# A hybrid layer on one core: zeros and an earlier norm at the start, the delta rule's masks applied where products are read, side work ranked anew

## The chip, the cores and the metric

The kernel runs on one core of one Trainium2 chip. Time is in microseconds (us) of the device, for the whole program. PE multiplies matrices (PEld, its weight loads, is shown apart), DVE, ACT and POOL work on tiles in SBUF and PSUM, SP issues the weight DMAs. Each engine runs its own instructions in the order of the program and waits on semaphores for the others.

## The reference

Two blocks with fp32 data: x has 256 tokens of 1024 channels. The first block is the one that changes:

```python
def hybrid_layer(x, norm_mix_w, w_in, ...):
    h = rmsnorm(x, norm_mix_w)
    proj = jnp.einsum("bsd,de->bse", h, w_in)
    qkv, z, b_logit, a_logit, lru_x, lru_gate = jnp.split(proj, SPLIT_IDX, axis=-1)
    qkv = jax.nn.silu(causal_depthwise_conv(qkv, gdn_conv_w))
    q, k, v = jnp.split(qkv, 3, axis=-1)          # 4 heads of 128, q and k l2-normalised
    beta = jax.nn.sigmoid(b_logit)
    g = -jnp.exp(gdn_A_log) * jax.nn.softplus(a_logit + gdn_dt_bias)
    o = gated_delta_rule_chunked(q, k, v, g, beta)
    gdn_out = rmsnorm(o, gdn_norm_w) * jax.nn.silu(z)
    xr = causal_depthwise_conv(lru_x, lru_conv_w) + lru_conv_b
    lru_out = rg_lru(xr, ...) * jax.nn.gelu(lru_gate)   # two gates, then a scan over the tokens
    x = x + jnp.einsum("bse,ed->bsd", jnp.concatenate([gdn_out, lru_out], -1), w_out)
    ...                                            # MLP: w_ff1, relu squared, w_ff2
```

The delta rule solves a unit lower triangular system per chunk and head, then carries a state from chunk to chunk:

```python
    a_low = jnp.where(strict, jnp.einsum("bhnid,bhnjd->bhnij", k_beta, k) * decay, 0.0)
    sol = lax.linalg.triangular_solve(a_low + eye, rhs, left_side=True, lower=True)
    ...
        v_new = u_c - jnp.einsum("bhck,bhkv->bhcv", w_c, state)
        o_c = (jnp.einsum("bhck,bhkv->bhcv", q_c * jnp.exp(g_c)[..., None], state)
               + jnp.einsum("bhij,bhjv->bhiv", attn_c, v_new))
```

The second block has two layers of gated MLPs, attention and a convolution branch, and is the same before and after.

## The kernel before

Everything is held with channels on partitions and the 256 tokens along the row. A weight product is made of three fp32r matmuls per k-tile of 128 channels: rounded weights by rounded x (L552), rounded weights by x's rest (L553), the weights' rest by rounded x (L554), each 128x256. ACT makes the rounded weights (`wh`, from `raw`, which a DMA brings), DVE the rest (`wl` = raw - wh); a table, POOLED, gives the rests of some jobs to POOL. A job is one output tile of 128 channels; it has eight k-tiles, so 24 matmuls.

The first block has 24 jobs of w_in: ORDER1 takes four tiles each of k, q, x (the LRU's input), g (its output gate), v and z. That is matmuls 1 to 576 of the weight stream. w_out follows in two parts: o1a, the four k-tiles that the LRU's result feeds (eight jobs of 12 matmuls), and o1b, those that the delta rule feeds. Both add into the same banks of PSUM. Then come the MLP and block two.

All else runs beside the jobs as **flows**, Python generators that yield between pieces: conv and SiLU of each tile (`conv4`, `do_qkv`), `decays` (beta and decays from w_ba), `sums` and `factors` (norms of q and k), `chunk` (the inverse of the triangular matrix and the state, one flow for each of two chunks of 128 tokens), `sides` (scaled q, k, v for it), `lru` (gates, square root, scan). A planner keeps a clock for each engine (`clk`) and calls `tick` behind each k-tile of a job: a flow goes on when its event has come, in order of its rank, and one with a limit only while DVE's clock is less than the limit ahead of PE's (`ready`, L372). So the planner writes down one fixed order for each engine. `force` lets flows run on where a job needs something.

In `chunk` the inverse T is built by levels: in each a product M1 of the masked matrix and T, a product with T, an addition, a transposition and a copy; the last blocks are 32 and 64 wide. The masks are LM, the masked matrix NL is made by POOL at L1110 (512 columns, once in each of four levels and two chunks). `lru` turns each of four tiles into two gates by products with LG and five ACT instructions. At the end the squares of the outputs are summed (`sso`), and norm and z's gate follow.

At the start ACT rounds x, four of the squares of x are made by ACT and four by POOL, POOL adds the halves, PE sums the columns by products with `ones`, and `root_norm` gives `rc`. `wb` is w_ba rounded and its rest, for the 32 products that give beta and the decays' input.

Helpers record an operation under their own line: ACT at L295, DVE at L307 (two tensors), L312/L314 (a tensor and numbers), L318 (scalar, tensor, tensor), POOL at L330, PE at L338 (products) and L342 (transpositions).

## Time and profile before

| | |
|---|---|
| time, median of 3 runs | 1510.01 us (1508.57 to 1511.97) |
| the profiled execution's own time | 1510.12 us |
| its span, first to last instruction | 1508.4 us |
| mean granted clock of PE | 0.991 |
| PE busy | 1471.4 us (98%) |
| DVE busy | 1073.8 us (71%) |
| ACT busy | 800.6 us (53%) |
| POOL busy | 136.7 us (9%) |

The profile is that of one execution. A row of the timeline gives start, duration, engine, line, operation, output and inputs, shape, how many instructions it joins, and in brackets the idle time ahead of it with the instruction that ended it. A row of a group gives busy time, mean ns of one, then idle time and its causes. In a joined row the first start and the whole length stand, and the ends of matmuls are modelled, so neighbouring rows overlap a little. The granted clock is 1.00 at full rate and 0.50 at half.

### The profile page before, as it was taken

How to read it: one execution, taken by the hardware profiler on the slowest of the kernel's cores; microseconds unless marked ns; L12 is line 12 of the kernel's file. 1: busy time of each engine (PE TensorE's matmuls, PEld its weight loads, DVE VectorE, ACT ScalarE, POOL GpSimd, SP SyncE). 2: the span in 40 equal slices, each digit the busy share in tenths (PEclk: the TensorE clock that was granted, in tenths of full speed). 3: DMA queues.
4: the chain of work that ended last, by engine and by line, in shares of the span. 5: the costliest groups of instructions: out<-in, count | busy, mean ns of one | idle time of the engine just before them, and what ended most of it. 6: DMA issues, size and time to landing. Idle time of an engine off the chain costs nothing. (4 is left out here: it accounts for less than half of the span.)

```text
span 1508.4 us, 29363 instructions
## 1 busy us (share of the span) xinstructions
PE 1471.4 (98%) x12130; PEld 1451.6 (96%) x12130; DVE 1073.8 (71%) x1910; ACT 800.6 (53%) x1349; POOL 136.7 (9%) x189
## 2 busy tenths in 40 slices
PE   7989999999999999999999999999999999999997
PEld 7888999999999999998999999999999989999997
DVE  5996877667666568998866655665568998876664
ACT  4568666544544445554554444544445556555552
POOL 2330300001000002231000000000002222000000
PEclk8999999999999999999999999999999999999998
DMA  5412455554644554333454444554454434555552
GB/s 207 163 57 73 164 205 190 187 200 145 209 170 176 178 177 144 144 134 112 147 214 171 173 169 161 199 185 174 165 190 155 164 113 140 184 207 196 189 183 76
DMA packets 36375, 248.57 MB, mean 165 GB/s; under 512 B 3984, under 2 KB 5264, under 8 KB 12304
## 3 DMA queue, kind: packets, MB, share of 16 engines
q1 hardware_dynamic: 35248, 245.50, 46.3%
q8 instruction: 95, 1.56, 0.4%
q10 hardware_dynamic: 992, 1.19, 0.2%
q14 instruction: 40, 0.33, 0.1%
HBM read 245.63 MB, written 1.05 MB: 164 GB/s over the span
## 5 line engine op out<-in xcount | busy, mean ns | idle before, releaser
L552 PE MATMUL bank<-x,wh 128*128 128x272 f32 (+1 forms) x2752 | 793.3, 288 | 11.0 <-ACT x L295 10.1
L553 PE MATMUL bank<-x,wh 128*128 128x272 f32 (+1 forms) x2752 | 782.8, 284 | 3.8 <-DVE x L318 2.2
L554 PE MATMUL bank<-x,wl 128*128 128x272 f32 (+1 forms) x2752 | 781.7, 284 | 4.4 <-DVE wl L307 4.4
L307 DVE TENSOR_TENSOR wl<-raw,wh 128x1024 fp32r<-128x1024 f32 (+3 forms) x467 | 546.6, 1172 | 182.7 <-PE bank L554 153.9
L295 ACT ACTIVATE wh<-raw 128x1024 fp32r<-128x1024 f32 (+4 forms) x494 | 492.1, 1001 | 255.3 <-issue 133.0
L552 PEld LDWEIGHTS bank<-x,wh 128*128 128x128 f32 x2752 | 521.5, 190 | 13.8 <-ACT x L295 10.5
L553 PEld LDWEIGHTS bank<-x,wh 128*128 128x128 f32 x2752 | 521.4, 189 | 6.9 <-DVE x L318 3.1
L554 PEld LDWEIGHTS bank<-x,wl 128*128 128x128 f32 x2752 | 521.9, 190 | 5.5 <-DVE wl L307 5.5
L554 PE MATMUL bank<-hid,wl 128*128 128x272 f32 (+1 forms) x960 | 270.5, 282 | 0.0
L552 PE MATMUL bank<-hid,wh 128*128 128x272 f32 (+1 forms) x960 | 270.5, 282 | 0.0
L553 PE MATMUL bank<-hid,wh 128*128 128x272 f32 (+1 forms) x960 | 270.5, 282 | 0.0
L553 PEld LDWEIGHTS bank<-hid,wh 128*128 128x128 f32 x960 | 180.5, 188 | 0.0
L554 PEld LDWEIGHTS bank<-hid,wl 128*128 128x128 f32 x960 | 180.5, 188 | 0.0
L552 PEld LDWEIGHTS bank<-hid,wh 128*128 128x128 f32 x960 | 180.5, 188 | 0.0
L307 DVE TENSOR_TENSOR tmp<-bank,R 128x272 f32<-128x272 f32 (+1 forms) x184 | 78.7, 429 | 63.5 <-PE bank L554 61.3
L295 ACT ACTIVATE tmp<-tmp 128x272 f32<-128x272 f32 (+1 forms) x140 | 59.4, 425 | 110.0 <-DVE tmp L307 78.0
L318 DVE SCALAR_TENSOR_TENSOR bank<-arena,C,bank 128x272 f32<-128x272 f32 (+1 forms) x232 | 102.3, 489 | 3.7 <-ACT bank L295 2.5
L510 POOL TENSOR_TENSOR wl<-raw,wh 128x1024 fp32r<-128x1024 f32 (+1 forms) x27 | 64.2, 2380 | 185.2 <-ACT wh L295 106.6
L307 DVE TENSOR_TENSOR hid<-tmp,hid 128x272 fp32r<-128x272 f32 (+1 forms) x120 | 51.7, 432 | 38.1 <-ACT hid L295 38.1
L295 ACT ACTIVATE hid<-tmp 128x272 fp32r<-128x272 f32 (+1 forms) x120 | 51.0, 426 | 42.3 <-DVE tmp L307 40.8
L295 ACT ACTIVATE x<-H,C 128x272 fp32r<-128x272 f32 (+2 forms) x64 | 30.0, 487 | 80.9 <-DVE H L307 80.3
L307 DVE TENSOR_TENSOR tmp<-tmp,bank 128x272 f32<-128x272 f32 (+1 forms) x88 | 38.0, 432 | 39.0 <-ACT tmp L295 39.0
(205 smaller groups left out, 883.2 us busy)
## 6 DMA issues: line engine op xcount, KB each, us to landing
raw<-in_w_dram SPq DMA_DIRECT2D x187, 1024.0 KB, 4.8
raw<-in_w_dram SPq DMA_DIRECT2D x32, 960.0 KB, 4.7
raw<-in_w_dram SPq DMA_DIRECT2D x16, 896.0 KB, 4.5
raw<-in_w_dram SPq DMA_DIRECT2D x2, 512.0 KB, 5.9
H<-in_xt_dram SPq DMA_DIRECT2D x1, 544.0 KB, 6.6
LG<-in_lgw_dram SPq DMA_DIRECT2D x1, 512.0 KB, 6.2
out_dram<-H SPq DMA_DIRECT2D x2, 256.0 KB, 2.2
LM<-in_cm_dram SPq DMA_DIRECT2D x1, 320.0 KB, 5.4
```

The source lines that it names most:

```text
L295: nc.scalar.activation(out, in_, func, scale=scale, **kw)
L307: nc.vector.tensor_tensor(out=out, in0=a, in1=b, op=fn)
L318: nc.vector.scalar_tensor_tensor(out=out, in0=a, scalar=s, in1=b, op0=op0, op1=op1)
L510: nc.gpsimd.tensor_tensor(out=lo[:, a:a + n], in0=raw[c][:, o:o + n], in1=wh[i][:, a:a + n].bitcast(F32), op=SUB)
L552: nc.tensor.matmul(acc, h[:, s], xh, start=first and done == 0, stop=False)
L553: nc.tensor.matmul(acc, h[:, s], xl, start=False, stop=False)
L554: nc.tensor.matmul(acc, lo[:, s], xh, start=False, stop=last and done == total - 1)
```

## The change

At the start, thirteen matmuls of zeros (128x512, bf16) run on PE, and in job 0 a further one behind each of seven products; job 0 takes its eight rounded products first, then the eight with the weights' rest, then the eight with x's rest. ACT makes all eight squares, nobody adds the halves, and PE sums all eight (16 products of one column instead of 8). The next weights are rounded ahead of the squares. The products for beta are turned round: 16 of 16x256 with x moving, and two small ones (`two`) that turn the sum back. `decays` starts earlier. The three zero columns of each conv tile are cleared once, in a ring of eight buffers, instead of once per tile. The conv of q is held back until k's factors and the decays are there, and q takes ACT's SiLU. Squares of q and k, the decay matrices DT and their scaling, all POOL's, go to ACT (`scales` is a new flow).

In `chunk`, k is turned once, for both kb and kx, instead of twice. The masks are transposed once (`masks`), M1 is the product with the unmasked matrix, and DVE applies the mask as it reads the product, where ACT copied it; NL and L1110 are gone. POOL makes no weight rests for w_in. Ranks: k's flows 0, q's 1.5, v's 1.7, x, g and z 2; LIMIT1 goes from 1.5 to 3.0, and the limit looks at ACT's clock too. `lru`'s gates become four flows of their own (`lru_gate`, rank 2), and the rests of its results are made in a second loop.

```diff
-POOLED = [..., (("o1b",), 2), (("K", "Q"), 8)]
-LIMIT1 = 1.5
+POOLED = [..., (("o1b",), 2)]
+LIMIT1 = 3.0
...
-        if f.limit is not None and clk["V"] > clk["P"] + f.limit:
+        if f.limit is not None and max(clk["V"], clk["A"]) > clk["P"] + f.limit:
...
+            if u == 0:
+                for w, part in ((h, x.hi), (lo, x.hi), (h, x.lo)):
+                    for i, k in enumerate(units[u][1]):
+                        nc.tensor.matmul(
+                            acc, w[:, 128 * i:128 * i + 128], part(k), ...
+                        )
+                        if w is h and part == x.hi and k < KD - 1:
+                            mm(free_banks[-1], zero[:, 0:128], zero)
...
+    for _ in range(WARM):
+        mm(free_banks[-1], zero[:, 0:128], zero)
...
     def squares():
-        yield "P"
-        for k in range(4):
-            act(SQ[1].f[:, k], X(4 + k), AF.Square)
-        cur[0].t, cur[0].eng = 0.0, "P"
-        for k in range(4):
-            pt(SQ[0].f[:, k], X(k), X(k), MUL)
-        for k in range(4):
-            pt(SQ[0].f[:, k], SQ[0].f[:, k], SQ[1].f[:, k], ADD)
...
+        for k in range(KD):
+            act(SQ[k // 4].f[:, k % 4], X(k), AF.Square)
         yield "P"
         yield from take()
-        root_norm([SQ[0].f[:, k] for k in range(4)], T1, rc)
+        root_norm([SQ[k // 4].f[:, k % 4] for k in range(KD)], T1, rc)
...
+    emit_high(1)
+    hop(start_flow(squares()))
...
-    def conv4(b, wname, t, out, state, bias=None):
+    def conv4(b, wname, t, out, state, bias=None, hold=()):
...
-        nc.gpsimd.memset(p[:, 5:8], 0.0)
         tt(p[:, 8:8 + T1], b[:, 0:T1], R[:, 0:T1], MUL)
         give(b)
+        if hold:
+            yield from wait(*hold)
...
-        yield from conv4(b, "gdn_conv_w", t, dst, "V" if t < 8 else "F")
+        yield from conv4(b, "gdn_conv_w", t, dst, "V", hold=[ev_fk, *ev_dec] if t < 4 else [])
+        if t < 4:
+            act(dst, dst, AF.Silu)
+        elif t < 8:
+            yield from twice_silu(dst, dst)
         if t < 8:
-            yield from twice_silu(dst, dst)
-            pt(SQ[t // 4].f[:, t % 4], dst, dst, MUL)
+            act(SQ[t // 4].f[:, t % 4], dst, AF.Square)
...
+        for k in range(KD):
+            mm(b[0:16, 0:T1], wb[:, k], xa.hi(k), k == 0, False)
+            mm(b[0:16, 0:T1], wb[:, k], xa.lo(k), False, k == KD - 1)
...
         for c in range(2):
-            for k in range(KD):
-                mm(b[:, 16 * c:16 * c + 16], xa.hi(k)[:, hs(c)], wb[:, k], k == 0, False)
-                mm(b[:, 16 * c:16 * c + 8], xa.lo(k)[:, hs(c)], wb[:, k, 0:8], False, k == KD - 1)
+            mm(b[:, 256 + 8 * c:264 + 8 * c], bas[0:16, hs(c)], two)
...
-            pt(DT[c].f, bh(tri), bc(G[:, 4 * c:4 * c + 4]), MUL)
+            for h in range(4):
+                act(DT[c].f[:, h], tri, AF.Copy, scale=G[:, 4 * c + h:4 * c + h + 1])
...
+    def masks():
...
+        for i in range(4):
+            tr(b[:, hs(i)], LM[:, 1 + i], ident)
+        cp(LM[:, 1:5], v4(b))
...
+    def scales(c):
+        yield from wait(ev_fk, ev_dec[c])
+        by_head(DT[c].f, DT[c].f, s16[:, 4 * c:4 * c + 4])
...
         for lev in range(1, 5):
-            nc.gpsimd.tensor_tensor(out=NL.f, in0=AT.f, in1=bh(LM[:, lev]), op=MUL)
...
             for h in range(4):
-                mm(b[:, hs(h)], NL.f[:, h], T.f[:, h])
-            cp(M1.f, v4(b))
+                mm(b[:, hs(h)], AT.f[:, h], T.f[:, h])
+            tt(M1.f, v4(b), bh(LM[:, lev]), MUL)
...
+    def lru_gate(t):
+        yield from wait(ev_room, ev_sp, *ev_q, ev_x[t])
...
         for t in range(4):
             tt(XR.f[:, t], XR.f[:, t], LQ.f[:, t], MUL)
             scan(LQ.f[:, t], LA.f[:, t], XR.f[:, t], 0.0, MUL, ADD)
             stt(GL.f[:, t], LQ.f[:, t], 0.5, GL.f[:, t], MUL, MUL)
-            yield from split(GL.f[:, t], mx.hi(4 + t), mx.lo(4 + t))
+            cp(mx.hi(4 + t), GL.f[:, t])
+            yield "V"
+        for t in range(4):
+            tt(mx.lo(4 + t), GL.f[:, t], mx.hi(4 + t).bitcast(F32), SUB)
...
-        start_flow(doers[c](b, off + t), *((0, LIMIT0) if c in "kq" else (2, LIMIT1)))
-        if i == 1:
-            start_flow(decays(), 1)
+        start_flow(doers[c](b, off + t), *{"k": (0, LIMIT0), "q": (1.5, LIMIT1), "v": (1.7, LIMIT1)}.get(c, (2, LIMIT1)))
+        if i == 0:
+            start_flow(decays(), 0.5)
...
             for c_ in range(2):
-                start_flow(sides(c_), 2)
-            start_flow(lru(), 2, LIMIT1)
+                start_flow(sides(c_), 1.6, LIMIT1)
+            for t_ in range(4):
+                start_flow(lru_gate(t_), 2, LIMIT1)
+            start_flow(lru(), 1.6, LIMIT1)
```

The order that the planner writes moves in three places that matter. First ACT at the start, from its roundings of x on (`x` from H, `arena` from H is squares, `wb` from C). Before:

```order
7 L295 ACTIVATE x00_117<-H_95,C_96 128x256 x8
8 L295 ACTIVATE arena_103<-H_95 128x256 x4
9 L295 ACTIVATE wb_136<-C_96 128x8x8
10 L295 ACTIVATE wh_198<-raw_131 128x1024
11 L295 ACTIVATE wh_200<-raw_134 128x1024
```

After:

```order
8 L297 ACTIVATE wh_183<-raw_133 128x1024
9 L297 ACTIVATE arena_103<-H_95 128x256 x8
10 L297 ACTIVATE wb_151<-C_96 128x8x8
11 L297 ACTIVATE wh_219<-raw_136 128x1024
12 L297 ACTIVATE wh_225<-raw_136 128x1024
```

The rounding of job 1's weights now stands ahead of the squares, which are eight; wb, on which DVE's next instruction waits in both kernels, stands behind them.

The second place is ACT from the first gate of the LRU on: a gate tile is two instructions that read a bank with `hb`, two with `n`, one with `p`; an `arena` copy from a bank of 512 columns is a step of the inverse. Before, two of the four tiles:

```order
94 L295 ACTIVATE tmp1_87<-bank2_80,hb_180 128x256
95 L295 ACTIVATE tmp2_88<-bank2_80,hb_180 128x256
96 L295 ACTIVATE arena_103<-tmp1_87,n4_177 128x256
97 L295 ACTIVATE arena_103<-tmp1_87,n8_178 128x256
98 L295 ACTIVATE tmp1_87<-tmp1_87,p4_179 128x256
99 L295 ACTIVATE arena_103<-bank4_82 128x512
100 L295 ACTIVATE arena_103<-arena_103,C_96 128x256
101 L295 ACTIVATE arena_103<-bank5_83 32x4x32 x2
102 L295 ACTIVATE arena_103<-bank7_85 128x512
103 L295 ACTIVATE tmp3_89<-bank3_81,hb_180 128x256
104 L295 ACTIVATE tmp4_90<-bank3_81,hb_180 128x256
```

After, the end of the fourth tile; the other three stand straight ahead of it, from row 106 on:

```order
121 L297 ACTIVATE tmp8_94<-bank3_81,hb_203 128x256
122 L297 ACTIVATE tmp2_88<-bank3_81,hb_203 128x256
123 L297 ACTIVATE arena_103<-tmp8_94,n4_200 128x256
124 L297 ACTIVATE arena_103<-tmp8_94,n8_201 128x256
125 L297 ACTIVATE tmp8_94<-tmp8_94,p4_202 128x256
126 L297 ACTIVATE arena_103<-bank6_84 128x512
127 L297 ACTIVATE arena_103<-bank2_80 128x512
128 L297 ACTIVATE tmp1_87<-arena_103 128x256
129 L297 ACTIVATE tmp6_92<-arena_103 128x256
130 L297 ACTIVATE arena_103<-bank5_83 32x4x32 x2
```

The four tiles stand in one block, and both chunks' last copies of T, rows 126 and 127, behind it.

The third place is PE around the last level of the inverse (L338 before and L340 after are products, with LG those of the gates; L342 and L344 transpositions; L552 to L554 and L567 to L569 weight matmuls). Before:

```order
499 L338 MATMUL bank0_78<-arena_103 128x128 x4
500 L342 MATMUL bank5_83<-M_97,arena_103 128x128 x4
501 L552 MATMUL bank6_84<-x00_117,wh_852 128x256
502 L553 MATMUL bank6_84<-x01_118,wh_852 128x256
503 L554 MATMUL bank6_84<-x00_117,wl_1001 128x256
504 L552 MATMUL bank6_84<-x00_117,wh_852 128x256
505 L553 MATMUL bank6_84<-x01_118,wh_852 128x256
506 L554 MATMUL bank6_84<-x00_117,wl_1001 128x256
507 L338 MATMUL bank7_85<-arena_103 128x128 x4
508 L338 MATMUL bank3_81<-arena_103 128x128 x4
509 L338 MATMUL bank2_80<-arena_103,LG_101 128x256 x2
```

After, from the last weight matmul of w_in on:

```order
658 L569 MATMUL bank6_84<-x00_117,wl_1164 128x256
659 L340 MATMUL bank1_79<-arena_103 128x128 x4
660 L340 MATMUL bank7_85<-arena_103 128x128 x4
661 L340 LDWEIGHTS zero_122
662 L340 MATMUL bank0_78<-zero_122 128x512
663 L340 MATMUL bank2_80<-arena_103 128x128 x4
664 L340 MATMUL bank5_83<-arena_103 128x128 x4
665 L340 MATMUL bank1_79<-arena_103,LG_101 128x256 x2
666 L340 MATMUL bank7_85<-arena_103,LG_101 128x256 x2
667 L340 MATMUL bank4_82<-arena_103,LG_101 128x256 x2
668 L340 MATMUL bank3_81<-arena_103,LG_101 128x256 x2
669 L344 MATMUL bank6_84<-M_97,arena_103 128x128 x4
```

Weight matmuls stood between such steps before; after, w_in has ended, and 28 rows of products and transpositions (659 to 686) follow each other until the first weight matmul of w_out.

More of the change, by code (lines that the diff above doesn't have):

```diff
@@ L702, in tile_hybrid_blocks @@
     warm = const.tile([128, 1], F32, name="warm")
+    zero = pool1.tile([128, 512], BF16, name="zero")
+    nc.gpsimd.memset(zero, 0.0)
     nc.gpsimd.memset(ones, 1.0)
@@ L748, in squares @@
         note(ev_r1)
+        act(warm, ones[:, 0:1], AF.Exp)
+        ts(hrc, rc, 0.5, MUL)
     def first_norm():
@@ L1092, in chunk @@
         used()
+        yield from wait(ev_scaled[c])
         tt(AT.f, v4(b), DT[c].f, MUL)
@@ L1272, in lru @@
+    def lru():
+        yield from wait(ev_x[0])
+        LA = lru_room["LA"] = yield from room(4, T1)
+        LQ = lru_room["LQ"] = yield from room(4, T1)
+        note(ev_room)
+        yield from wait(*ev_gate, *ev_g)
         act(LQ.f, LQ.f, AF.Sqrt, scale=0.25)
@@ L1346, in tile_hybrid_blocks @@
         if m == 0:
-            force(lambda: not [f for f in flows if f.gen.__name__ in ("chunk", "lru", "decays", "factors", "sides")])
+            force(lambda: not [f for f in flows if f.gen.__name__ in ("chunk", "lru", "decays", "factors", "sides", "scales", "lru_gate")])
     mx.done()
```

146 lines of the change are left out of this document (86 added, 60 removed).

## The prediction

> **What bounds the kernel now.** I read first the busy shares, then the table of stretches. Its columns: the stretch in us, its length, then busy time (instructions) of PE, PEld, DVE, ACT and POOL, granted clock, DMA share, GB/s.
>
> ```profile
> 0.00:7.15 7.15, 0.00 (x0) 0.00 (x1) 0.02 (x1) 3.10 (x5) 1.02 (x8) 1.00 0.73 257
> 7.15:18.20 11.05, 8.44 (x44) 7.49 (x44) 11.03 (x13) 8.12 (x16) 6.44 (x11) 0.97 0.79 282
> 18.20:31.63 13.43, 13.43 (x79) 13.24 (x79) 4.99 (x27) 3.49 (x8) 0.00 (x0) 0.64 0.32 135
> 31.63:70.00 38.37, 36.22 (x300) 34.86 (x300) 35.49 (x81) 19.20 (x33) 12.63 (x21) 1.00 0.44 156
> 70.00:140.10 70.10, 64.58 (x627) 61.62 (x626) 56.45 (x107) 51.98 (x115) 17.10 (x19) 1.00 0.22 78
> 140.10:161.00 20.90, 20.37 (x158) 18.08 (x156) 15.90 (x44) 14.18 (x43) 0.00 (x0) 1.00 0.14 51
> 161.00:190.00 29.00, 29.00 (x247) 29.00 (x247) 24.93 (x39) 21.24 (x43) 13.88 (x11) 1.00 0.62 218
> ```
>
> The reader is to see that PE is the bound nearly everywhere. The last weight matmul of w_in (number 576 of the stream) runs at 140.1, number 648 at 161.0; from there PE is busy without a gap, and the order behind it is the same in both kernels but for bank numbers. So one number decides: **when does number 648 run**, 161.0 now. Up to it PE is busy 8.44 + 13.43 + 36.22 + 64.58 + 20.37 = 143.0 us and idle 18.0, of which 7.15 are the wait for the first data. There is little to win by cutting waits, 8 us between 31.63 and 161; and PE work that leaves w_in for later is won only if it runs without waits there.
>
> DVE is near its limit from 31.63 to 70 (35.49 of 38.37), and part of that isn't its own work:
>
> ```profile
> L318 DVE SCALAR_TENSOR_TENSOR arena<-arena,C 128x256 f32<-128x256 f32 x48 | 30.5, 645 | 5.8 <-ACT arena L295 5.4
> 58.89 0.48 DVE L318 SCALAR_TENSOR_TENSOR arena<-arena,C 128x256 f32<-128x256 f32 x1
> 89.70 1.43 POOL L1110 TENSOR_TENSOR arena<-arena,LM 128x512 f32<-128x512 f32 x1 [2.18 <-PE bank L338]
> 89.93 1.49 DVE L318 SCALAR_TENSOR_TENSOR arena<-tmp,tmp 128x256 f32<-128x256 f32 x1
> ```
>
> The conv step takes 0.48 us clean and 0.645 in the mean of 48, so 48 x 0.165 = 8 us of waiting in this group alone; the 1.49 us one lies exactly over a POOL instruction that ends at 91.13. [...]
>
> **The opening.** It is PE's 31.6 us now.
>
> ```profile
> 6.59 3.45 ACT L295 ACTIVATE x<-H,C 128x256 fp32r<-128x256 f32 x8 [0.35 <-DMA H<-in_xt_dram]
> 9.95 1.32 ACT L295 ACTIVATE arena<-H 128x256 f32<-128x256 f32 x4
> 11.32 2.93 ACT L295 ACTIVATE wh<-raw 128x1024 fp32r<-128x1024 f32 x3
> 14.56 0.21 DVE L307 TENSOR_TENSOR wb<-C,wb 128x64 fp32r<-128x64 f32 x1
> 14.70 3.48 DVE L307 TENSOR_TENSOR wl<-raw,wh 128x1024 fp32r<-128x1024 f32 x3
> 15.96 0.39 PE L554 MATMUL bank<-x,wl 128*128 128x256 f32 x1 [0.53 <-DVE wl L307]
> 16.18 2.15 PE L338 MATMUL bank<-ones,arena 128*128 128x1 f32 x16
> 24.10 3.77 PE L338 MATMUL bank<-wb,x 128*128 128x16 f32 x32
> 17.60:21.00 3.40, 3.40 (x17) 3.40 (x18) 2.59 (x8) 2.76 (x5) 0.00 (x0) 0.50 0.92 388
> 21.00:24.40 3.40, 3.40 (x19) 3.40 (x18) 0.00 (x0) 0.16 (x1) 0.00 (x0) 0.50 0.44 186
> 53.65 1.84 PE L338 MATMUL bank<-ones,arena 128*128 128x1 f32 x16
> ```
>
> The zeros let PE be busy before the data come, and job 0's new order lets it run while DVE still makes the low parts. But job 1's third product (at 15.96 now) needs a rounding rest that stands on DVE behind the small wb rest, and that waits for ACT: 8 roundings of x to 10.0, one weight rounding 0.98 (2.93 for three), now 8 squares at 0.33 (1.32 for four) = 2.64, and wb, about DVE's 0.21: 13.9; DVE's 0.21 and 1.16 for the weight (3.48 for three) lead to 15.2. That is 0.8 earlier, no more. The sums of squares then are 32 passes instead of 16 (nobody adds the halves any more): 15.3 + 2 x 1.84 = 19.0 at full clock. The 32 narrow ba passes at 24.10 become 16 wide ones, x moving.
>
> The clock decides the rest. It stood at 0.50 from 17.6 to 24.4, just behind the narrow passes of 16.18. If it does so again, 20 of the 32 passes run before 17.6 and 12 at 0.23 to 20.4; then 21 weights and 16 ba products: 19 at 0.21 to 24.4, 18 at 0.117, and 0.5 for the small rows: **27.0**. At full clock all along: 19.0 + 37 x 0.117 + 0.5 = 23.8. I take 27.0, since the narrow passes have doubled.
>
> **The stretch of w_in after job 1** has 22 jobs, 528 matmuls; 29.00 / 247 = 0.117 each gives 61.8. Side products between them:
>
> ```profile
> 104.64 1.95 PE L338 MATMUL bank<-arena 128*128 128x128 f32 x16
> 108.45 1.05 PE L338 MATMUL bank<-arena 128*128 128x128 f32 x8
> 106.78 0.60 PE L342 MATMUL bank<-M,arena 128*128 128x128 f32 x4
> 107.22 1.03 PE L338 MATMUL bank<-arena,LG 128*128 128x256 f32 x4
> 39.71 1.96 PE L338 MATMUL bank<-arena,ones 128*128 128x512 f32 x4
> ```
>
> A further group of four products costs 1.95 - 1.05 = 0.90, four transposes 0.44 (106.78 to 107.22). The new order has 16 such groups and 15 groups of transposes here (k is turned twice instead of four times, the masks once more), two sums of 1.84 and the decays' 2.0: 14.4 + 6.6 + 3.7 + 2.0 = 26.7. DVE keeps pace, but not by much: 91.9 busy now (35.49 + 56.45), less at least 8 of blocking, plus 8 mask products at 0.69 (as the bank product at 156.19 below) and one weight of 1.16, less the LRU's scans and their neighbours, which go behind (4 x 1.5 and 8 x 0.4, an estimate from the same 128x256 forms at 0.4 to 0.7): 81 of the 88.5 that the stretch has. So the end of w_in is 27.0 + 61.8 + 26.7 = **T = 115.5**, against 140.1. The order shows what that costs: the last level of the inverse, all four gates, V, the last blocks and the state come behind it with no weights to cover them.
>
> **The tail from T to number 648.** ACT's line counts here:
>
> ```profile
> 108.60 0.84 ACT L295 ACTIVATE tmp<-bank,hb 128x256 f32<-128x256 f32 x2
> 110.96 1.07 ACT L295 ACTIVATE arena<-bank 128x512 f32<-128x512 f32 x2
> 122.97 1.70 ACT L295 ACTIVATE arena<-bank 32x128 f32<-32x128 f32 x6
> 130.40 0.76 ACT L295 ACTIVATE arena<-bank 64x256 f32<-64x256 f32 x2
> 134.02 1.28 ACT L295 ACT_TABLE_LOAD   x1
> 135.32 1.07 ACT L295 ACTIVATE arena<-arena 128x1024 f32<-128x1024 f32 x1
> 138.84 0.40 ACT L295 ACTIVATE x<-arena 128x256 fp32r<-128x256 f32 x1
> 141.85 2.16 ACT L295 ACTIVATE arena<-bank,hbeta 128x128 f32<-128x128 f32 x8
> 150.18 0.27 ACT L295 ACTIVATE junk<-bank 128x128 f32<-128x128 f32 x1
> 151.77 0.16 DVE L307 TENSOR_TENSOR sso<-sso,fq 128x4 f32<-128x4 f32 x1 [3.54 <-ACT junk L295]
> 152.98 0.38 PE L338 MATMUL bank<-zero 1*128 1x512 bf16 x1
> 154.22 0.16 DVE L307 TENSOR_TENSOR sso<-sso,fq 128x4 f32<-128x4 f32 x1
> 156.19 0.69 DVE L307 TENSOR_TENSOR arena<-bank,sso 128x512 f32<-128x512 f32 x1
> ```
>
> - Two M1 groups, DVE's two masks, two groups for T, and the first gate product behind them on PE: 1.8 + 0.6 + 1.8 + 1.0 + 0.2 of handover = T + 5.4. There ACT's gates start: 108.60 to 110.96 is 2.36 per tile, four make 9.4, with the table 10.7: T + 16.1. Now they lie among w_in's weights; here they stand **ahead of the copies of T**, so the delta rule waits for them.
> - Then ACT alone has two copies of 0.5 (110.96), eight narrow ones of 0.28 (122.97), four of 64 partitions at 0.38 (130.40), V's eight (2.16), the square root with its table 2.3 (134.02, 135.32), U, w and S at 0.5, and six of 0.37 for the LRU and its neighbours (138.84): 1.0 + 2.2 + 1.5 + 2.2 + 2.3 + 1.5 + 2.2 = 12.9. With 2.2 of handovers at the state, an estimate of four times the 0.5 to 0.6 by which a group's reader starts behind its end: T + 31.2, where the outputs of chunk 0 are ready.
> - The four squares 1.6 (150.18 to 151.77), DVE's chain 2.6 (151.77 to 154.38), then norm, gate, a weight rest and two LRU rests, five of 0.4 to 0.7, 2.7; ACT's rounding of chunk 0's result, 0.6, stands **ahead of chunk 1's squares**, 1.6; their short chain and norm 2.0 with handovers, and the last LRU rest 0.4. That is T + 42.9 with 0.2 between.
> - That rest holds the first w_out tile at its fourth weight, number 586. The other 62 take 7.3, the three rows of zeros among them 1.1 (0.38 at 152.98): T + 51.3 = 166.8.
> - PE idles from about T + 7 to T + 16, and the rows at 17.60 show what follows on thin work. Groups at half clock cost 0.9 more each; I take 2 us, between 0 and 5 (three groups on the path and a half-rate start of the weights). So 168.8.
>
> [...]
>
> 168.8 - 161.0 = +7.8. The profiled execution took 1510.12 (span 1508.4), which is 0.1 from the median of 1510.01, so the time is **1517.9**.
>
> **Rivals.** A difference under 0.2%, 3.0 us, is about what a measurement of this kernel can't tell from no change.
> 1. *PE's clock stays full and its groups are cheap.* The opening ends at 23.8 (-3.2), the tail loses no 2. 1517.9 - 5.2 = 1512.7, and with groups at 0.83 (-1.1) and transposes at 0.36 (-1.2) 1510.4: no change. For it: after 31.2 the clock is 1.00 in every stretch. Against: the narrow passes are doubled. Chance 0.2.
> 2. *Faster: ACT never starves in the tail.* Its own work there is 10.7 + 12.9 + 1.6 + 0.5 (U) + 0.5 (a weight) + 0.6 + 1.6 = 28.4; I charge it 35.1 (T + 5.4 to T + 40.5). If the two chunks' steps fill each other's handovers, 6.7 goes; on rival 1's base that is 1503.7. It decides from 3.3 us of waits saved on. For it: the chunks are independent up to the state, and ACT was busy 14.18 of 20.90 in the stretch from 140.1 without PE waiting. Against: PE had weights there to fill with, and the state's steps hang on each other. Chance 0.17.
> 3. *Slower yet: the opening gives nothing,* job 1's product coming at 15.96 as now (+0.8) and half clock lasting one row of 3.4 us longer (+1.7), and the tail loses the 5 of the clock's upper end (+3): 1523.4. Chance 0.13.
> 4. *The change doesn't do what it says:* DVE, with POOL's weight and masks on it, is no freer, so PE waits in w_in as now (2.15 + 5.52 = 7.7 us): at most 1525.6. For it: the 81 of 88.5. Chance 0.05.
>
> My own case has 0.45, with 1514 to 1521 as its range. Faster is rival 2 and a little of rival 1 (0.2); no change most of rival 1 (0.2); slower the rest (0.6). The range leaves out the far half of rival 2 and of rival 3: 1506 to 1523.
>
> **What would show it.** Right: w_in's last matmul near 115, POOL idle, conv steps at 0.48 throughout; then PE idle for some 20 us between 115 and 158, ACT full with gates from about 121 to 131, copies of T behind them, and number 648 near 169. Wrong: gates that run before T, PE busy over 80% from T on, or w_in ending after 120 with DVE as what PE waits for. The opening is right if the sums of squares end at 19 to 21 and half clock covers them.

## The result, and the profile after

| | before | after |
|---|---|---|
| time, median (4 runs each) | 1509.29 us (1508.05 to 1511.97) | 1531.83 us (1531.46 to 1538.3) |
| ratio after/before | | 1.0154, 95% interval 1.0137 to 1.0172 |
| the profiled execution's own time | 1510.12 us | 1531.46 us |
| its span | 1508.4 us | 1529.7 us |

The change costs 22.5 us. The forecast was 1517.9, with 1506 to 1523 as its range: the sign was right, the size was not. One execution of a later kernel, the profiled one of warm_gap, ran at a mean granted clock of 0.75 and took 1852.5 us; it is left out of every median and ratio below.

The page of the changed kernel, its span, the busy time of each engine and the granted clock in 40 slices of 38 us:

```profile
span 1529.7 us, 29361 instructions
PE 1484.8 (97%) x12150; PEld 1461.9 (96%) x12150; DVE 1063.9 (70%) x1914; ACT 806.8 (53%) x1371; POOL 103.3 (7%) x152
PEclk8997899999999999999999999999999999999998
```

The slice with a 7 is that from 115 to 153 us. The loss lies around it. Below, **the marker** is the start of the row of zeros that PE runs directly behind number 648 of the weight stream; from there the order is the same in all kernels. First the kernel before, then the changed one, PE's rows with the marker as the last:

```profile
160.69 0.39 PE L338 MATMUL bank<-zero 1*128 1x512 bf16 x1
```

```profile
161.14 0.38 PE L568 MATMUL bank<-x,wh 128*128 128x256 f32 x1 [2.37 <-DVE x L309]
161.48 3.50 PE L340 MATMUL bank<-arena 128*128 128x128 f32 x16
170.97 0.58 PE L568 MATMUL bank<-x,wh 128*128 128x256 f32 x1 [5.01 <-DVE x L309]
181.76 0.39 PE L340 MATMUL bank<-zero 1*128 1x512 bf16 x1
```

The marker comes 21.1 us later, the span is 21.3 longer. The table of stretches, before and then after (stretch, length, busy time and instructions of PE, PEld, DVE, ACT, POOL, then granted clock, DMA share, GB/s):

```profile
100.00:120.00 20.00, 19.42 (x191) 18.64 (x191) 15.34 (x24) 14.46 (x29) 4.63 (x5) 1.00 0.15 54
120.00:140.00 20.00, 19.32 (x238) 18.22 (x232) 13.89 (x32) 18.87 (x41) 0.13 (x2) 1.00 0.29 107
140.00:160.00 20.00, 19.47 (x153) 17.53 (x152) 15.00 (x43) 13.30 (x42) 0.00 (x0) 1.00 0.15 53
```

```profile
29.20:122.00 92.80, 90.08 (x758) 88.50 (x757) 73.82 (x175) 56.26 (x123) 2.20 (x2) 0.98 0.34 124
120.00:140.00 20.00, 11.50 (x106) 10.32 (x107) 14.20 (x34) 15.05 (x31) 0.00 (x0) 0.86 0.00 0
140.00:160.00 20.00, 16.18 (x166) 14.76 (x161) 8.44 (x25) 15.03 (x45) 0.00 (x0) 0.63 0.01 2
160.00:180.00 20.00, 13.85 (x80) 12.81 (x81) 9.68 (x22) 5.24 (x15) 0.00 (x0) 0.74 0.15 52
```

w_in now ends at 122.0 instead of 140.1, and up to there PE is busy 90.08 of 92.80. That part of the change does what it says: POOL's share falls from 9% to 7%, and the conv steps run clean. The group of conv steps after, 486 ns in the mean where 645 stood before:

```profile
L320 DVE SCALAR_TENSOR_TENSOR arena<-arena,C 128x256 f32<-128x256 f32 x48 | 21.5, 486 | 1.4 <-ACT arena L297 1.3
```

But the 18 us won by 122 are lost twice over by 182: in 60 us PE is busy 41.5, and its clock is 0.63 to 0.86 where it was full. What PE waits for up to 230 us (engine, line, what it waits for: total, times, longest; the three largest of seven rows):

```profile
PE bank L340 <- ACT arena L297: 13.4, 5, 8.5
PE bank L568 <- DVE x L309: 7.4, 2, 5.0
PE bank L569 <- DVE wl L309: 2.5, 1, 2.5
```

The first of these is the forecast's own wait (gates ahead of the copies of T, 8.5, and 2.3 in w_in). The second is a wait of w_out's first tile for **the rests of the LRU's result** (`mx.lo`, the x's rest of three of its four k-tiles). DVE's rows show where those rests stand:

```profile
149.83 0.42 DVE L309 TENSOR_TENSOR x<-arena,x 128x256 fp32r<-128x256 f32 x1
158.14 0.16 DVE L309 TENSOR_TENSOR sso<-sso,fq 128x4 f32<-128x4 f32 x1 [7.90 <-ACT junk L297]
160.67 0.42 DVE L309 TENSOR_TENSOR x<-arena,x 128x256 fp32r<-128x256 f32 x1
161.60 0.42 DVE L309 TENSOR_TENSOR x<-arena,x 128x256 fp32r<-128x256 f32 x1
170.50 1.02 DVE L309 TENSOR_TENSOR x<-arena,x 128x256 fp32r<-128x256 f32 x2
```

The LRU's scans are over at 149.5 and the first rest follows at 149.83. Then DVE is idle for 7.90 us: the next instruction in its order is the norm of chunk 0's output, which waits for ACT's squares, and the second and third rest stand behind it. The last one stands behind chunk 1's norm. PE's rows above close the loop: the weight that waits for the rest (2.37 us, up to 161.14) stands ahead of the 16 products of chunk 1's state and output at 161.48; so the wait for chunk 0's norm delays chunk 1's outputs, these delay its norm, and that delays the last rest.

### The profile page after: what moved, and what is told of

Its sections match the earlier page's. It is cut to its first block, busy times and chain, and to the rows that moved or that the text cites. A ratio compares the mean times of both kernels' runs of the same rounds, so it can differ in the third digit from the quotient of the medians.

```text
span 1529.7 us, 29361 instructions
## 1 busy us (share of the span) xinstructions
PE 1484.8 (97%) x12150; PEld 1461.9 (96%) x12150; DVE 1063.9 (70%) x1914; ACT 806.8 (53%) x1371; POOL 103.3 (7%) x152
## 5 line engine op out<-in xcount | busy, mean ns | idle before, releaser
L567 PE MATMUL bank<-x,wh 128*128 128x272 f32 (+1 forms) x2744 | 788.7, 287 | 3.4 <-ACT x L297 3.0
L569 PE MATMUL bank<-x,wl 128*128 128x272 f32 (+1 forms) x2744 | 778.1, 284 | 2.5 <-DVE wl L309 2.5
L309 DVE TENSOR_TENSOR wl<-raw,wh 128x1024 fp32r<-128x1024 f32 (+4 forms) x468 | 545.8, 1168 | 192.7 <-PE bank L569 160.0
L568 PEld LDWEIGHTS bank<-x,wh 128*128 128x128 f32 x2744 | 518.7, 189 | 12.9 <-DVE x L309 9.8
L567 PEld LDWEIGHTS bank<-x,wh 128*128 128x128 f32 x2744 | 518.9, 189 | 5.5 <-ACT x L297 3.2
L569 PEld LDWEIGHTS bank<-x,wl 128*128 128x128 f32 x2744 | 518.9, 189 | 2.7 <-DVE wl L309 2.7
L569 PE MATMUL bank<-hid,wl 128*128 128x272 f32 (+1 forms) x960 | 270.5, 282 | 0.0
L567 PE MATMUL bank<-hid,wh 128*128 128x272 f32 (+1 forms) x960 | 270.5, 282 | 0.0
L568 PEld LDWEIGHTS bank<-hid,wh 128*128 128x128 f32 x960 | 180.6, 188 | 0.0
L567 PEld LDWEIGHTS bank<-hid,wh 128*128 128x128 f32 x960 | 180.5, 188 | 0.0
L569 PEld LDWEIGHTS bank<-hid,wl 128*128 128x128 f32 x960 | 180.5, 188 | 0.0
L512 POOL TENSOR_TENSOR wl<-raw,wh 128x1024 fp32r<-128x1024 f32 (+1 forms) x26 | 60.9, 2343 | 280.8 <-PE bank L569 214.4
```

What stands on the lines that cost most here:

```text
L309: nc.vector.tensor_tensor(out=out, in0=a, in1=b, op=fn)
L512: nc.gpsimd.tensor_tensor(out=lo[:, a:a + n], in0=raw[c][:, o:o + n], in1=wh[i][:, a:a + n].bitcast(F32), op=SUB)
L567: nc.tensor.matmul(acc, h[:, s], xh, start=first and done == 0, stop=False)
L568: nc.tensor.matmul(acc, h[:, s], xl, start=False, stop=False)
L569: nc.tensor.matmul(acc, lo[:, s], xh, start=False, stop=last and done == total - 1)
```

## The experiments

Each kernel's edit is against the changed kernel, or against the kernel before where that is said. Each ratio goes by runs of the kernel before made beside it. "Last rest" is the start of the LRU's fourth rest on DVE in the profiled execution; "row at" gives the start of a row that joins several rests, and the fourth starts within 1.6 us behind it.

| kernel | time, median (range) | ratio, 95% interval | last rest | marker |
|---|---|---|---|---|
| before (the profiled run) | 1510.12 | 1 | 147.8 | 160.7 |
| after | 1531.83 (1531.46–1538.3) | 1.0154 (1.0137–1.0172) | 170.5 | 181.8 |
| limit15 | 1533.75 (1530.2–1537.4) | 1.0146 (1.0111–1.0181) | row at 168.1 | 180.9 |
| ranks_kq | 1531.48 (1527.5–1532.5) | 1.0133 (1.0098–1.0169) | row at 164.6 | 177.7 |
| old_rules | 1530.86 (1526.4–1533.2) | 1.0123 (1.0088–1.0159) | row at 164.0 | 176.9 |
| rest_early | 1535.43 (1530.4–1537.1) | 1.0139 (1.0105–1.0173) | 168.4 | 180.6 |
| old_rules_rest | 1530.07 (1527.6–1533.3) | 1.0133 (1.0112–1.0154) | 167.4 | 178.3 |
| ranks_kq_rest | 1528.22 (1527.5–1532.7) | 1.0126 (1.0105–1.0147) | row at 164.9 | 177.4 |
| opening_alone | 1527.14 (1519.7–1531.2) | 1.0099 (1.0062–1.0136) | 143.4 | 152.2 |
| masks_alone | 1525.77 (1522.2–1531.1) | 1.0101 (1.0067–1.0136) | 161.0 | 172.0 |
| opening_masks | 1534.23 (1527.9–1537.5) | 1.0132 (1.0094–1.0169) | row at 167.6 | 179.1 |
| rest_late | 1517.33 (1514.7–1520.7) | 1.0035 (1.0016–1.0053) | 154.9 | 166.6 |
| lru_first | 1524.79 (1519.3–1525.9) | 1.0089 (1.0059–1.0118) | 154.1 | 169.4 |
| masks_lru_first | 1513.52 (1508.7–1521.2) | 1.0025 (1.0007–1.0042) | 152.8 | 164.9 |
| opening_masks_first | 1515.97 (1514.1–1524.2) | 1.0049 (1.0031–1.0066) | 156.0 | 166.7 |
| ranks_kq_first | 1513.81 (1510.5–1522.0) | 1.0023 (0.9998–1.0048) | 152.6 | 163.3 |
| split_early | 1527.46 (1520.7–1531.3) | 1.0111 (1.0079–1.0143) | 161.2 | 172.0 |
| split_early_v | 1519.30 (1516.6–1521.9) | 1.0064 (1.0049–1.0079) | 154.7 | 170.6 |

The marker tells the kernels apart better than the time does, since the part behind it has a spread of its own of some 6 us (last section).

### Is it the order of the inverse and the gates?

The forecast's reason: inverse, gates and state come behind w_in with no weights to cover them. Three kernels move them forward again, by the old limit, the old ranks of the conv flows, or both with the old rule.

```diff
 limit15:
-LIMIT1 = 3.0
+LIMIT1 = 1.5
 ranks_kq:
-... *{"k": (0, LIMIT0), "q": (1.5, LIMIT1), "v": (1.7, LIMIT1)}.get(c, (2, LIMIT1)))
+... *((0, LIMIT0) if c in "kq" else (2, LIMIT1)))
 old_rules: both, and
-        if f.limit is not None and max(clk["V"], clk["A"]) > clk["P"] + f.limit:
+        if f.limit is not None and clk["V"] > clk["P"] + f.limit:
```

> Changed kernel with LIMIT1 back at 1.5, nothing else. By its order the inverse of both chunks is then done at weight matmul 552 instead of behind 576, but three of four gates still stand behind 576. Theory 'order' (the inverse, gates and state lie behind w_in with nothing to cover them, and that is the loss): the end of w_in comes later by the products moved into it (about 9 us) and the tail shrinks by more, PE idle in it falls from about 28 to 15 us, time 1515 to 1520. Theory 'clock' (half clock in the tail costs most): gain only as far as PE idles less, 1525 to 1529. Theory 'new forms' (masks on DVE, q's SiLU, squares on ACT make the steps themselves longer): no gain, 1530 to 1534.

> Changed kernel with the conv flows' old ranks and limits (k and q 0 with the limit 5, the others 2), LIMIT1 at 3.0. All four gates and both inverses then stand before 576. Theory 'order': the best of the three, tail of about 25 us, time 1505 to 1512. Theory 'clock': about the same as 'order' here if PE no longer idles, so this run alone doesn't part these two. Theory 'new forms': 1527 or more, since every step is as before.

> Changed kernel with the old ranks of the conv flows, LIMIT1 at 1.5 and the limit on DVE's clock alone; the new arithmetic and the new opening stay. Theory 'order': gates before 576 but the 64-wide blocks behind; between the two other runs or as good as the better, 1507 to 1515. Theory 'new forms': 1527 or more.

The inverse did come forward. In limit15 its 32-wide blocks start at 114.4 instead of 139.1, and yet the marker is at 180.9 instead of 181.8; old_rules and ranks_kq gain 4 to 5 us of the 21. The waits of PE in limit15 say why:

```profile
PE bank L568 <- DVE x L309: 9.9, 3, 8.4
```

The gap that was filled came back as a longer wait for the LRU's rests: 9.9 us instead of 7.4. So the order theory names a loss, but not what sets the end. All three times fell where the theory 'new forms' (the steps themselves are longer: 1530 to 1534 for limit15, 1527 or more for the others) had put them. That theory doesn't hold either: further down, lru_first has the same steps and is 7 us faster, and ranks_kq_first, with all of them, has its marker 2.6 us behind that of the kernel before.

### Which part of the change does it?

The change is cut into its parts, on the kernel before: the opening alone (zeros, order of job 0, ACT's squares, early norm, beta's products turned round, decays earlier); the masks alone (no NL, DVE's mask products); both.

```diff
 masks_alone, against before:
-            nc.gpsimd.tensor_tensor(out=NL.f, in0=AT.f, in1=bh(LM[:, lev]), op=MUL)
...
-                mm(b[:, hs(h)], NL.f[:, h], T.f[:, h])
-            cp(M1.f, v4(b))
+                mm(b[:, hs(h)], AT.f[:, h], T.f[:, h])
+            tt(M1.f, v4(b), bh(LM[:, lev]), MUL)
```

> Kernel before with the opening of the change alone: zeros, job 0's order, squares on ACT, sums of 16 products, beta's products turned, decays early. POOL, ranks, chunk and LRU as before. If the opening is worth what its clock lets it be: first conv input about 2 us earlier, 1506 to 1509. If the doubled narrow sums at half clock eat it: 1509 to 1513.

> Kernel before with the opening and the masks applied on DVE as M1 is read (masks turned once, POOL's product gone); ranks, limits, q, k's turns and the LRU as before. By its order both inverses are done at weight 438 and all gates before 576. If POOL's masks were what held the chain, the chain ends early and the time is 1498 to 1505; if the new reading is itself slow, 1510 to 1520.

> Kernel before with the masks alone: turned once by PE, applied by DVE as M1 is read, no POOL product, opening and LRU as before. By its order the state's first products stand at 564 to 576 and the LRU's gates at 441 to 531. If POOL's blocking of DVE was worth 8 us and more: 1500 to 1506. If the end of the chain is set by ACT and DVE's hand-overs behind w_in: 1507 to 1515.

Each part alone makes the kernel 1% slower, and not by what it adds. With the opening alone the marker is at 152.2, **8.5 us earlier** than before, and the loss, 18 us in the profiled execution (1519.7 us, the fastest of its four), comes behind it:

```profile
152.22 0.39 PE L339 MATMUL bank<-zero 1*128 1x512 bf16 x1
168.74 1.97 PE L343 MATMUL bank<-M,arena 128*128 128x128 f32 x8 [4.05 <-DVE arena L308]
172.22 0.58 PE L566 MATMUL bank<-x,wh 128*128 128x256 f32 x1 [1.51 <-ACT x L296]
```

There the weight stream runs ahead of the delta rule: 64 of the delta rule's products run from 156.3 to 164.7 and its result is turned at 168.74, all behind number 648, and o1b waits for that result until 172. With the masks alone it is the other way: the delta rule comes first, and the LRU's last rest, at 161.0, holds the stream (marker 172.0). In the kernel before both ends meet: the last LRU rest is at 147.8, the delta rule's last rest at 161.1, the marker at 160.7. By these traces the old order was in balance, and each edit that shifts the planner's clocks gives up one end of it. That is a reading of three traces; no run tests it by itself.

### Are the rests late because they are made in a second loop?

The change makes all four rounded results of the LRU first and the rests after. rest_early undoes that in the changed kernel; rest_late does only that in the kernel before; the two other kernels join the undoing with the old ranks and rules.

```diff
 rest_late, against before (rest_early is the reverse, against after):
-            yield from split(GL.f[:, t], mx.hi(4 + t), mx.lo(4 + t))
+            cp(mx.hi(4 + t), GL.f[:, t])
+            yield "V"
+        for t in range(4):
+            tt(mx.lo(4 + t), GL.f[:, t], mx.hi(4 + t).bitcast(F32), SUB)
```

> Changed kernel, only the LRU's loop as before: each tile's rest is made right behind its rounding instead of in a second loop. PE's order is the same but for a few weight matmuls. Theory 'rest held' (in the changed kernel and in the three with other ranks w_out's first tile waits on a rest of the LRU that stands on DVE behind the chain of the output norm, so that its 62 weights run bare behind it): the weights fill PE's gaps between 156 and 171 and the time falls by 5 to 8 us, to 1524 to 1527. Theory 'total latency' (the delta rule's chain itself ends too late; o1b waits for it anyway): 1530 to 1533.

> Kernel before with one thing of the change: the LRU's rests in a second loop. By its order the state's products then stand between matmuls 576 and 585 of the stream, behind w_in, as in the changed kernel. Theory 'rest held': w_out's first weights wait for the rests and the tail is bare, 1515 to 1522. Theory 'total latency': 1509 to 1512.

> Changed kernel with the old ranks and limits and the LRU's rests made early, so both suspects at once. In old_rules the state ended about as early as in the kernel before (output squares 150.9 to 158.2, there 150.2 to 153.6), but the LRU's last rest came at 164 and w_out's 62 weights ran bare behind it. Theory 'rest held' on top of 'order': these weights go into the gaps, 1512 to 1520. Theory 'total latency': 1527 to 1532.

> As the run above but LIMIT1 3.0 and the limit on ACT's clock too; the conv flows' ranks as before and the rests early. Theory 'rest held' with 'order': 1512 to 1520. Theory 'total latency': 1526 to 1531.

'Rest held' was right for rest_late, whose time lies in its 1515 to 1522, and missed in the other three; two of them, old_rules_rest and ranks_kq_rest, fell where 'total latency' had put them. In the kernel before, the edit alone costs 0.35% and puts the rests where the changed kernel has them, in and behind chunk 0's norm. DVE's rows of rest_late:

```profile
145.37 0.42 DVE L307 TENSOR_TENSOR x<-arena,x 128x256 fp32r<-128x256 f32 x1
150.53 0.42 DVE L307 TENSOR_TENSOR x<-arena,x 128x256 fp32r<-128x256 f32 x1
152.07 0.41 DVE L307 TENSOR_TENSOR x<-arena,x 128x256 fp32r<-128x256 f32 x1
154.89 0.41 DVE L307 TENSOR_TENSOR x<-arena,x 128x256 fp32r<-128x256 f32 x1
```

The last rest moved from 147.8 to 154.9, and the marker from 160.7 to 166.6. But in the changed kernel undoing it gains nothing: three rests come early there, and the planner still puts the fourth behind the norms, at 168.4 (in this kernel the fourth tile's scan itself stands behind chunk 0's norm). So the loop isn't the cause; what the kernels so far share is the place behind the norm, whatever put it there. In all kernels up to here but opening_alone, the marker comes 11 to 13 us behind the fourth rest, or the row that holds it (62 weights at 0.117 and three rows of zeros at 0.38, the paces of the trace of before at full clock, are 7.3 + 1.1 us and so most of that).

### The place itself, taken away

One line in `chunk`, ahead of the squares of the outputs, tells the planner to write the LRU's rests down first. Nothing else is changed: same instructions, another order.

```diff
-        yield from wait(ev_fq)
+        yield from wait(ev_fq, *[mx.ev[4 + i] for i in range(4)])
         so = sso[:, sc]
```

> Changed kernel with one wait added to the planner: the squares of the delta rule's outputs are not placed before the LRU's rests. Over ten kernels the 648th matmul comes 10 to 13 us behind the last rest of the LRU (147.8 to 160.7 before, 170.5 to 181.8 in the changed kernel). Theory 'LRU's last rest': the rests come at about 150 to 152, the scans being done at 149.5, w_out's weights run in PE's gaps and the 648th comes at 163 to 172, bounded by the delta rule's result at 170 or so: 1513 to 1521. Theory 'total latency' (delta rule alone sets the end): 1527 to 1532.

> Kernel masks_alone with the same wait added. There the state's outputs came 10 us earlier than in the kernel before (140.7) but the LRU's last rest at 161, behind the output norm. Theory 'LRU's last rest': rests by about 150, 648th matmul at 158 to 163, time 1505 to 1512. Theory 'total latency': 1520 to 1526.

> Kernel opening_masks with the same wait. LRU's last rest there at about 166, state's outputs at 152. Theory 'LRU's last rest': rests by about 152, time 1505 to 1514. Theory 'total latency': 1527 to 1535.

> Kernel ranks_kq_rest with the same wait. Theory 'LRU's last rest': rests by about 152, the delta rule's result at about 163, 648th matmul at 163 to 167, time 1511 to 1518. Theory 'total latency': 1526 to 1531.

It gains in each of four kernels: by the medians 7 us for after, 12 for masks_alone, 18 for opening_masks, 14 for ranks_kq_rest; by the marker 12.4, 7.1, 12.4 and 14.1. The theory 'LRU's last rest' had the direction in all four and the time in one: ranks_kq_first lies in its range, the three others 1.5 to 4 us above theirs, while 'total latency' missed all four by 2 to 12 us. In lru_first the rests and PE's rows read:

```profile
148.36 0.75 DVE L309 TENSOR_TENSOR x<-arena,x 128x256 fp32r<-128x256 f32 x2
150.15 0.43 DVE L309 TENSOR_TENSOR x<-arena,x 128x256 fp32r<-128x256 f32 x1 [0.44 <-ACT x L297]
154.08 0.42 DVE L309 TENSOR_TENSOR x<-arena,x 128x256 fp32r<-128x256 f32 x1 [3.50 <-ACT x L297]
160.15 0.16 DVE L309 TENSOR_TENSOR sso<-sso,fq 128x4 f32<-128x4 f32 x1 [5.64 <-ACT junk L297]
```

```profile
137.65 1.12 PE L340 MATMUL bank<-arena 32*32 32x32 f32 x32 [8.51 <-ACT arena L297]
169.39 0.39 PE L340 MATMUL bank<-zero 1*128 1x512 bf16 x1
```

The same blocks in after:

```profile
139.12 1.12 PE L340 MATMUL bank<-arena 32*32 32x32 f32 x32 [8.50 <-ACT arena L297]
```

All four rests now stand ahead of the norm, and no wait of PE for them is left. The gap in front of the 32-wide blocks is the same 8.5 us. From those blocks to the marker it is 169.39 - 137.65 = 31.7 us, where after has 181.76 - 139.12 = 42.6: **10.9 us go with that one line**. The other 1.5 by which the marker is earlier come from the opening, with the same instructions (last section).

With the conv flows' old ranks as well, and the rests in the first loop, the marker is at 163.3: 6.1 more, with the gates and the inverse among w_in's weights again. This step changes two things at once, so it doesn't part them. 2.6 us to the kernel before are left. So of the marker's 21.1, on this path: 12.4 up to lru_first, 6.1 by ranks and loop, 2.6 by the rest. On another path the parts differ, since the old ranks alone gave 4.1 (ranks_kq) and the line on top of ranks_kq_rest gave 14.1.

### A shorter opening

PE's longest wait in the opening, 2.5 us for a weight's rest, is taken out of ranks_kq_first: `emit_split(1)` makes it ahead of the squares. split_early_v has the old rule of the limit as well.

```diff
     emit_high(1)
+    emit_split(1)
     hop(start_flow(squares()))
```

> ranks_kq_first with one line more: job 1's weight rest is made ahead of the squares and of the small rest wb, so that TensorE's wait for it in the opening (2.5 us in the trace of the changed kernel) goes. Theory A (time is set by when the LRU's last rest comes, not by where w_in ends): the opening is some 2 us shorter, but the gates come later in the order (behind weight 576), so the marker stays between 162 and 166 and the time within 3 us of ranks_kq_first's 1513.8. Theory B (each us won at the start is won at the end): marker at 161 and a time of 1511 to 1512.

> split_early with the old rule of the limit (it looks at VectorE's clock alone), which brings the LRU's gates forward to weights 537 to 549 of the stream and lets the delta rule's last state fall into the first 30 weights of w_out. Theory A: the last LRU rest comes some 3 us earlier than in split_early, marker at 159 to 163, time 1508 to 1513, the best of all variants and level with the kernel before. Theory B (only the length up to the end of w_in counts): the same as split_early within 2 us.

Both theories missed: 1527.5 and 1519.3, markers 172.0 and 170.6. PE's waits in split_early show that nothing was won even locally:

```profile
PE bank L340 <- ACT arena L297: 12.3, 6, 4.9
PE bank L340 <- DVE two L309: 2.7, 1, 2.7
PE bank L340 <- DVE arena L309: 2.3, 1, 2.3
```

The wait for the weight's rest became one for `two`, the next small thing that DVE has to make; everything behind was planned anew, the gates fell behind weight 576 once more, and the last rest came at 161.2. So these two don't price the opening's wait, and that price stays open. They show again that moving one instruction can cost some 9 us of order further down (marker 163.3 to 172.0). In split_early_v the marker is 15.9 us behind the last rest, as it is 15.3 in lru_first: where something else holds w_out, the rule of 11 to 13 us ends.

### Is it the clock?

From 140 to 180 the changed kernel has a granted clock of 0.63 and 0.74. Were these 20-us stretches all PE's own time, the loss would be 7.4 + 5.2 us. Two kernels add products of zeros to keep PE busy over the gap between 130 and 139, and over the one ahead of the last rest.

```diff
 warm_tail, against after:
+    def heat(n):
+        for _ in range(n):
+            nc.tensor.matmul(free_banks[-1], zero[:, 0:128], zero, start=True, stop=True)
...
+            if lev == 4 and c == 1:
+                heat(36)
...
+        if c == 0:
+            heat(20)
 warm_gap: free_banks[0], heat(36), heat(3) at the narrow blocks and the state, heat(10) last
```

> Changed kernel with its order kept and 36 matmuls of zeros behind the last transpositions of T (about 7.7 us of PE where it idles 8.5 us) and 20 behind the transpositions of chunk 0's result (4.3 us in a gap of 5 us), so that PE doesn't idle there; it only adds work that nothing reads. Theory 'clock': the tail from 139 on runs at full clock, the groups of the state at 0.9 instead of 1.75 each and the first w_out weights at 0.117 instead of 0.21, time down by 4 to 7 us to 1525 to 1528. Theory 'order' with my own price of 2 us for the clock: 1529 to 1530. If the clock halves on narrow work rather than on idle time, no change or slower: 1531 to 1534.

> Changed kernel, order kept, with zeros that wait for nothing: 36 behind T's last transpositions (PE idles 8.5 us there), 3 behind each narrow step of chunk 1 and behind the first state, 10 behind the transpositions of chunk 0's result. In the run warm_tail the zeros went to a bank that ACT still read, so they ran behind the gap and not in it. Theory 'clock' (of the 20.7 us that the 648th matmul comes later, half rate between 134 and 175 is 6 to 9): 1523 to 1528, granted clock in the tail near 1.00. Theory 'idle only': 1530 to 1535.

Neither time tells it: both are longer than every theory had given. In warm_tail the zeros' bank was one that ACT still read, so the first 36 ran behind the gap, as work added to the path (PE's row, L1113 being the zeros):

```profile
140.74 9.44 PE L1113 MATMUL bank<-zero 128*128 128x512 bf16 x35 [8.51 <-ACT arena L297]
```

It took 1540.66 us, ratio 1.0192 (1.0162–1.0221). warm_gap used a free bank and added zeros at the narrow blocks too: 1538.74 us as the median of three, 1.0168 (1.0125–1.0211); its only trace is that of the 1852.5 us execution and isn't read here.

The second 20 zeros of warm_tail did run in the gap ahead of the last rest, at 176.01, and there the trace does tell something. Its weight that waits for that rest, and its marker:

```profile
181.30 0.39 PE L568 MATMUL bank<-x,wh 128*128 128x256 f32 x1 [0.70 <-DVE x L309]
190.14 0.39 PE L340 MATMUL bank<-zero 1*128 1x512 bf16 x1
```

From that weight to the marker it takes 8.8 us, where after has 181.76 - 170.97 = 10.8: 2.0 us are half clock behind the wait (after's granted clock is 0.50 from 170.97 to 175). That parts the 10.9 us of lru_first, as an estimate from rows of three traces. The two waits for the rests are 2.37 + 5.01 = 7.4. The 16 products behind the first wait take 3.50 in after (at 161.48) and 1.95 in lru_first (at 158.34), so 1.5. With the 2.0 that is 10.9: 7.4 of waiting and 3.5 of slower products. The state's small blocks don't enter, since the clock is near half there in both (from 140 to 156.3 it is 0.55 in after and 0.58 in lru_first). How the 6.1 divides, and what the narrow blocks' clock costs, **stays open**.

## Why the prediction failed, step by step

- **Opening, 27.0; measured 29.2 (+2.2).** The weight's rest came at 14.98 (15.2 forecast), so the wait was right, and half clock behind it too. But it covered more: all 32 one-column sums, which ended at 22.2 instead of 20.4, and the products for beta. PE's rows of after (granted clock 0.50 from 14.8 to 25.1):

```profile
14.98 0.58 PE L569 MATMUL bank<-x,wl 128*128 128x256 f32 x1 [2.50 <-DVE wl L309]
15.36 6.82 PE L340 MATMUL bank<-ones,arena 128*128 128x1 f32 x32
22.82 3.05 PE L340 MATMUL bank<-x,wb 128*16 128x256 f32 x16
```

  Some 1.6 of the 2.2 depend on the execution: limit15 and lru_first, with the same instructions up to there, took 4.62 and 4.86 us for those sums and ended the opening 1.6 us earlier. With 1.84 us for 16 sums at full clock (before, at 53.65) and 6.82 for 32 at half, their half clock began at about 17.7 and 17.4, an estimate, near where the forecast had put it (17.6). What decides which of the two an execution gets, these traces don't show.

- **w_in, 88.5 us from there to T; measured 92.8 (+4.3).** DVE kept pace, as the step said: 73.8 of 92.8; the 8 us of blocking that it took off came too, as 48 conv steps x (645 - 486) ns = 7.6. What was missed stands on ACT. q's SiLU is held back, and two tiles of it with their squares, a table load ahead, stand in front of the scaling of the turned k; PE waits 2.33 for that, and a clock of 0.50 follows from 89.9 to 93.3. Over the 92.80 PE is idle 2.7, and a clock of 0.98 loses some 1.9; together that is about the 4.3. The sign given for this, a w_in that ends after 120 with DVE as what PE waits for, came half true: it ended at 122, and PE waited 0.4 us for DVE. ACT's rows, then PE's:

```profile
85.88 1.28 ACT L297 ACT_TABLE_LOAD   x1
87.18 1.62 ACT L297 ACTIVATE arena<-arena 128x256 f32<-128x256 f32 x4
89.01 1.12 ACT L297 ACTIVATE arena<-bank,fx 128x128 f32<-128x128 f32 x4
```

```profile
90.18 2.08 PE L340 MATMUL bank<-arena 128*128 128x128 f32 x8 [2.33 <-ACT arena L297]
```

- **The tail, T + 53.3; measured T + 59.7 (+6.4).** This is the step that failed most. Its first half is right to the microsecond: gates start at T + 5.7 (5.4 forecast) and the copies of T stand behind them, at T + 16.5 (16.1):

```profile
127.73 0.82 ACT L297 ACTIVATE tmp<-bank,hb 128x256 f32<-128x256 f32 x2
138.50 1.06 ACT L297 ACTIVATE arena<-bank 128x512 f32<-128x512 f32 x2
156.54 0.28 ACT L297 ACTIVATE junk<-bank 128x128 f32<-128x128 f32 x1 [0.30 <-PE bank L340]
```

  The squares of chunk 0 begin at T + 34.5 (31.2 forecast, +3.3): the small blocks between run at a clock of 0.55 (140 to 156.3), for which I took 2 us out of a range of 0 to 5. The last LRU rest comes at T + 48.5, with the weight it holds at T + 49.0 (42.9 forecast): another 2.8. The step saw that the rest stands behind the norms and that w_out waits for it. It did not see that the weights of that same tile stand ahead of chunk 1's products on PE, so that the wait for rest two is paid again in rest four. The rest of the stream took 10.8 instead of 8.4, its first 4 us at half clock (0.50 from 170.97 to 175; PE's rows: 0.41 a pass at 173.06, 0.28 from 175.70), and the 2 us for the clock had been meant for both: 6.1 + 2.4 - 2 = 6.5.

The three steps add to 2.2 + 4.3 + 6.4 = 12.9, and the forecast missed the profiled execution by 1531.5 - 1517.9 = 13.6. Of the 0.7 between, 0.3 is the base (161.0, where the marker of before is at 160.7) and the rest lies behind the marker. **So the step that failed is a matter of size**: the side work moved behind w_in into a bare tail as forecast, but the tail's term, T + 53.3, measured T + 59.7, and w_in's 88.5 measured 92.8. Outside the opening the clock was given 2 us in all, and each wait was counted once. Two waits were not in the mechanism: PE's for the k behind q's SiLU (2.33), and the loop by which the wait for the rests is paid twice (2.37 and 5.01). The range failed with them: its upper end came from clock terms of 3 to 5 us in single places, and the losses came in all three at once, each with a wait of PE ahead of its half clock (2.50, 2.33 and 8.50 us).

Of the rivals, the first (full clock) and the second (ACT never starves) are refuted by the stretches above. The third had the right direction, but its 1523.4 had no term for the rests. The second's own condition, ACT never short of work, fails too: in the 20 us from 160 it is busy 5.24. The fourth is refuted: DVE was freed, and behind job 1 PE waits in w_in 0.4 us for it, where it was 4.6.

The larger lesson is in the runs. The forecast's "tail" was treated as a given of the change. It isn't: 10.9 us of it hang on which of two ready flows the planner writes first, and one line gives them back. No kernel here beats the one before; ranks_kq_first, with most of the change kept, comes to 1.0023 (0.9998–1.0048).

What brings half clock, this trace doesn't tell: the 0.55 from 140 to 156.3 stands behind an 8.5 us gap, but PE's blocks there are narrow too, so it doesn't part idleness from thin work. The forecast's 2 us for the clock held a half-rate start of w_out's weights, which no run of the kernel before shows; after showed one in its place, 0.50 from 170.97 to 175, worth 2.0 of those 10.8.

## What to carry to other kernels

Where a planner writes fixed orders, look for the last producer of the next weight tile on each in-order engine, and for what it stands behind. A result that is ready can sit there behind a wait for another chain, and where the consumer's queue also feeds that chain, the wait is paid twice: here 2.4 and 5.0 us. Moving an inverse forward by 25 us was worth 1 us here; moving three 0.4-us instructions ahead of a wait was worth 10.9. And price half clock as one case for all the thin terms together, not as a small addend in each: here one execution had 0.50 from 14.8 to 25.1, 0.50 from 89.9 to 93.3 and 0.55 from 140 to 156.3.
